# Linear ReLU attention on one Trainium2 core: K's masked copies split in halves, and loads issued seven octets ahead instead of nine

## The chip, the cores and the metric

The kernel runs on one core of one Trainium2 chip. The metric is the device time of one execution in microseconds (us), as the median of several executions.

## The reference

For each of 8 x 12 = 96 heads, with sequence length 512 and head dimension 64, in fp32:

```python
Q_feat = np.maximum(0, Q)
K_feat = np.maximum(0, K)
KV = np.einsum('bhkd,bhkv->bhdv', K_feat, V)
K_sum = np.sum(K_feat, axis=2)
numerator = np.einsum('bhqd,bhdv->bhqv', Q_feat, KV)
denominator = np.einsum('bhqd,bhd->bhq', Q_feat, K_sum)
return numerator / (denominator[:, :, :, None] + 1e-10)
```

## The kernel before

The 96 heads are handled as 12 groups of 8 heads, called octets and numbered 0 to 11. Of each octet, Q, K and V are 1 MB each in HBM (fp32), and so is the output. One transfer moves one of these to or from SBUF, laid out as 128 partitions of 32 rows of 64 numbers. There are thus 36 loads and 12 stores of 1 MB each. The loads of octets 1 to 11, and Q's of octet 0, convert to bf16 on the way; K and V of octet 0 come in fp32 into two buffers that later serve as output buffers.

Two queues issue transfers. GpSimd (POOL) issues nearly all loads, in `load` and `load_q`: K, V, Q of each octet, but K, Q, V for the last one. Its transfers use six semaphores in turn, so each issue waits until the transfer six places earlier has landed. SyncE (SP) issues K and V of octet 0 at the start, and stores. `AHEAD` says how many octets are loaded before the first step; it is also the number of buffers (`NI`) for each of Q, K and V. After that, step i handles the normalisation of octet o = i - 1, then the store of octet o, then the load of octet o + AHEAD + 1 if there is one. `store` (L246) puts the store on POOL's queue, in front of those loads, while there are loads to come; otherwise it goes to SP's queue, and the first of SP's stores waits for K of octet 11 to land. There are seven output buffers (`NOUT`), used in turn, so the normalisation of octet o overwrites the buffer of octet o - 7 and waits for that octet's store to have landed (octets 7 to 11; octets 5 and 6 follow the two buffers that held the fp32 inputs).

Each engine has its own fixed order of instructions, and waits on semaphores that the class `Order` works out from the keys that each operation reads and writes. TensorE (PE) runs a hand-written loop, `products` (L350). In step i, for octet i, with the octet before finished along the way:

1. PE transposes Q of octet i (L360), in two halves; ScalarE (ACT) applies the ReLU to them (L209).
2. PE multiplies K's masked copies with V's (L369), 64 matmuls, the first 32 of which use rows 0 to 15 of the octet's 32 rows (the first half) and the last 32 rows 16 to 31. Each half ends with a signal. ACT copies the product out (L217).
3. PE transposes the previous octet's product back (L378), two halves of 8.
4. PE computes denominators (L354, the form with 16 columns), then the two halves of the numerators (L354, 256 columns). These overwrite the PSUM tiles that step 3 filled, so they wait for VectorE's two normalisations of the previous octet. ACT copies the numerators out (L225; in the last step VectorE takes one half).

VectorE (DVE) in step i, in this order:

- `copy_q(i + 1)` (L206): copies Q of the next octet to the tile that PE transposes; it waits for that Q to land.
- `prep_k(i + 1, 0)` and `prep_k(i + 1, 1)` (L189): ReLU of the next octet's K times a mask, one copy for even and one for odd heads, into the single tile `kf`. Each covers all 32 rows and waits until PE's matmuls of item 2 have read the tile to the end.
- `norm(i - 1, 0)`, `norm(i - 1, 1)` (L239): divides the previous octet's numerators, PSUM to the output buffer.
- three small instructions for the denominators (L230, L234, L237).
- `prep_v` of the next octet (L202), two instructions; ACT does a third (L200).

The key of a K copy stands for a whole copy, which is what makes it wait for both halves of the matmuls:

```python
KF = [[("kf", 0), ("kf", 1), ("vo", 0, j), ("vo", 1, j), "vo1"] for j in range(2)]
```

Of the kernel before, what the change touches and what calls it, by code (L numbers as in the profile page):

```python
# [96 lines left out]
def kernel(  # L97
# [14 lines left out]
    R = S * 4 // P  # L112
# [1 line left out]
    U = RQ // 2  # L114
    NO = NH // 8
    assert NO * 8 == NH and R == 16 and RQ == 32
    AHEAD = 9
    NI = AHEAD
    NOUT = 7
    LANES = 6  # L120
# [16 lines left out]
    mask = sb.tile([P, 2, 2], fp32, name="mask")  # L137
    mask_h = sb.tile([P, 8, 2], fp32, name="mask_h")
    kf = sb.tile([P, RQ, 2, D], bf16, name="kf")
    vo = sb.tile([P, RQ, 2, D4], bf16, name="vo")  # L140
# [22 lines left out]
    def lane(who):  # L163
        turn[who] += 1
        return lanes[who][(turn[who] - 1) % len(lanes[who])]

    do = Order(nc, sems)

    def kv_src(o):
        if o == 0:  # L170
            return (o_sb[0], ("o", 0)), (o_sb[1], ("o", 1))
        return [(x[o % NI].rearrange("p (r d) -> p r d", d=D), (n, o % NI)) for n, x in (("k", k_sb), ("v", v_sb))]
# [6 lines left out]
    def load(o):  # L179
        i = o % NI  # L180
        for n, X, t in (("K", Kr, k_sb), ("V", Vr, v_sb)):
            if n == "V" and o == NO - 1:
                load_q(o)
            do.op("pool", lambda e: e.dma_start(out=t[i], in_=X[o], single_packet=True), writes=[(n.lower(), i)],  # L184
                  dma=lane("pool"))
        if o < NO - 1:
            load_q(o)

    def prep_k(o, s):  # L189
        src, key = kv_src(o)[0]  # L190
        do.op("dve", lambda e: e.tensor_scalar(kf[:, :, s, :], src, scalar1=0.0, scalar2=mask[:, 0, s:s + 1],  # L191
                                               op0=Alu.max, op1=Alu.mult),
              reads=[key, ("mask", 0)], writes=[("kf", s)])

    def prep_v(o, t, halves, who, sem=None):
        src, key = kv_src(o)[1]
        rs = slice(R * halves[0], R * halves[-1] + R)
        to, src, m = vo[:, rs, t, 2:D + 2], src[:, rs], mask[:, 1, t:t + 1]
        if who == "act":
            make = lambda e: e.activation(to, src, Act.Copy, scale=m)  # L200
        else:
            make = lambda e: e.tensor_scalar(to, src, scalar1=m, scalar2=None, op0=Alu.mult)  # L202
        do.op(who, make, reads=[key, ("mask", 1), "vo1"], writes=[("vo", t, j) for j in halves], sem=sem)

    def copy_q(o):
        do.op("dve", lambda e: e.tensor_copy(q2, q_sb[o % NI]), reads=[("q", o % NI)], writes=["q2"], sem="q2")  # L206

    def relu_q(j):
        do.op("act", lambda e: e.activation(qt[:, j * (U // 2):(j + 1) * (U // 2)], ps_qt[j], Act.Relu),  # L209
              reads=[("pq", j)], writes=[("qt", j)])  # L210
# [3 lines left out]
    def evac_kv():  # L214
        for s in range(2):
            for c in range(2):
                do.op("act", lambda e: e.copy(  # L217
                    kvd[64 * c:64 * c + 64, s:8:2, c * D1:c * D1 + D1].rearrange("p (g t) d -> p g t d", t=2),
                    ps_kv[64 * s:64 * s + 64, :, 0:2 * (D + 2)].rearrange(
                        "p g (t d) -> p g t d", t=2)[:, :, :, c:c + D1]),  # L220
                    reads=[("pk", 0), ("pk", 1)], writes=[("kvd", s, c)], sem="ev" if s + c == 2 else None)
# [6 lines left out]
    def denominators():  # L228
        ps = ps_den.rearrange("p (u h c) -> p u (h c)", u=U, h=8)
        do.op("dve", lambda e: e.scalar_tensor_tensor(  # L230
            own.rearrange("p u h c -> p u (h c)"), ps, 1e-10,
            mask_h.rearrange("p h c -> p (h c)").unsqueeze(1).to_broadcast([P, U, 16]), op0=Alu.add, op1=Alu.mult),
            reads=["pd", "mask_h"], writes=["own"])
        do.op("dve", lambda e: e.tensor_reduce(  # L234
            out=den.rearrange("p (u c) -> p u c", c=2), in_=own.rearrange("p u h c -> p u c h"), op=Alu.add,
            axis=mybir.AxisListType.X), reads=["own"], writes=["den"])
        do.op("dve", lambda e: e.reciprocal(rec, den), reads=["den"], writes=["rec"])  # L237

    def norm(o, j):  # L239
        i = (o + 2) % NOUT  # L240
        rs = slice(16 * j, 16 * j + 16)
        do.op("dve", lambda e: e.tensor_tensor(o_sb[i][:, rs], ps_x[j].rearrange("p (r d) -> p r d", d=D),  # L242
                                               rec[:, rs].unsqueeze(2).to_broadcast([P, 16, D]), op=Alu.mult),
              reads=[("x", j), "rec"], writes=[("o", i, j)] if i > 1 else [("o", i, j), ("o", i)], sem=f"n{j}")

    def store(o):  # L246
        i = (o + 2) % NOUT
        to, src = Or[o], o_sb[i].rearrange("p r d -> p (r d)")
        keys = [("o", i, h) for h in range(2)]
        if o + AHEAD + 1 < NO:  # L250
            do.op("pool", lambda e: e.dma_start(out=to, in_=src, single_packet=True), reads=keys, dma=lane("pool"))
        else:
            keys.append(("k", (NO - 1) % NI))
            do.op("sp", lambda e: e.dma_start(out=to, in_=src), reads=keys,
                  dma=lane("sp" if o + NOUT < NO else "last"), kept=o + NOUT >= NO)

    KF = [[("kf", 0), ("kf", 1), ("vo", 0, j), ("vo", 1, j), "vo1"] for j in range(2)]
    PK = [("pk", 0), ("pk", 1)]
    QT = [("qt", 0), ("qt", 1)]
    OT = [("ot", 0), ("ot", 1)]  # L260
# [4 lines left out]
    def body():  # L265
# [12 lines left out]
        for h in range(4):  # L278
            for t in range(2):
                memset("pool", mask[32 * h:32 * h + 32, 1, t:t + 1], 1.0 if h % 2 == t else 0.0,  # L280
                       [("m", h, t), ("mask", 1)])
        for o in range(1, AHEAD + 1):
            load(o)
# [8 lines left out]
    def setup():  # L292
        do.op("dve", lambda e: e.tensor_copy(ident32, ident), reads=["ident"], writes=["ident32"])
        for c in range(2):
            do.op("dve", lambda e: e.tensor_reduce(
                out=mask_h[:, :, c], in_=ident32.rearrange("p (h b) -> p h b", h=8), op=Alu.add,
                axis=mybir.AxisListType.X), reads=["ident32"], writes=[("mh", c), "mask_h"])
        do.op("dve", lambda e: e.tensor_reduce(
            out=mask[:, 0, :], in_=mask_h[:, :, 0].rearrange("p (a s) -> p s a", s=2), op=Alu.add,
            axis=mybir.AxisListType.X), reads=["mask_h"], writes=[("mask", 0)])  # L300
        prep_k(0, 0)
        prep_k(0, 1)
        prep_v(0, 1, (0,), "act", "a0")
        prep_v(0, 0, (0, 1), "dve", "d0")
        prep_v(0, 1, (1,), "dve", "d1")
        do.op("dve", lambda e: e.memset(kvf.bitcast(fp32)[:, 0:4 * D1], 0.0), writes=KVD, sem="n0")
        do.op("dve", lambda e: e.memset(kvf.bitcast(fp32)[:, 4 * D1:], 0.0), writes=KVD, sem="n1")
        copy_q(0)
        for j in range(2):
            nc.scalar.sem_inc(sems[f"t{j}"], 1)  # L310
            do.note("act", "act", (), (), f"t{j}", 1)

    def step(i):
        r = i + 1
        more, last = i + 1 < NO, i == NO

        if not last:
            do.looped([("q2", r)], ["q2", "ident"], [("pq", 0)])
            do.looped([], ["q2", "ident"], [("pq", 1)])
            relu_q(0)  # L320
            relu_q(1)
            do.looped([("a0", r), ("d0", r)], KF[0], PK + ["pd"])
            do.looped([("d1", r)], KF[1], PK + ["pd"])
            evac_kv()
            if more:
                prep_v(i + 1, 1, (0,), "act", "a0")
                copy_q(i + 1)
                prep_k(i + 1, 0)
                prep_k(i + 1, 1)
        if i > 0:  # L330
            o = i - 1
            do.looped([("t0", r), ("t1", r)], [*OT, "ident32"], [("x", 0)])
            do.looped([], [*OT, "ident32"], [("x", 1)])
            for j in range(2):
                norm(o, j)
            store(o)
            if o + AHEAD + 1 < NO:
                load(o + AHEAD + 1)
        if not last:
            do.looped([("ev", r)], [*QT, *KVD], ["pd"])  # L340
            denominators()
            for j in range(2):
                do.looped([(f"n{j}", r)], [*QT, *KVD], [("x", j)])
            copy_ot(0, "act")
            copy_ot(1, "act" if more else "dve")
            if more:
                prep_v(i + 1, 0, (0, 1), "dve", "d0")
                prep_v(i + 1, 1, (1,), "dve", "d1")
# [85 lines left out]
```

## Time and profile before

| | |
|---|---|
| time, median of 3 runs | 125.53 us (125.38 to 125.61) |
| the profiled execution's own time | 125.56 us |
| its span, first to last instruction | 123.7 us |
| mean granted TensorE clock | 0.944 |
| busy, share of span: PE, DVE, ACT, POOL | 69%, 67%, 63%, 22% |
| HBM read, written | 37.75 MB, 12.58 MB: 407 GB/s over the span |
| chain that ended last | DMA 71%, PE 8%, DVE 7%, issue 5%, POOL 4% |

The span is cut in 40 slices of 3.09 us. In the rows of the page each digit is the busy share of one slice in tenths. The row GB/s counts bytes at the SBUF side: a load that turns fp32 into bf16 counts half of what it reads from HBM, so 212 there stands for 424 GB/s read from HBM, while a store counts in full. A row of a group reads: line, engine, operation, tile written and tiles read, shapes, number of instructions, then busy time and mean ns of one, then the engine's idle time in front of them and who ended it.

### The profile page before, as it was taken

Reading aid. Unit: us, or ns where it says so; the run is one execution under the profiler, and the core shown is the slowest. Engines: PE = TensorE matmul, PEld = TensorE weight load, DVE = VectorE, ACT = ScalarE, POOL = GpSimd, SP = SyncE. Lnnn points to the kernel's source line nnn. Section 1 sums busy time; section 2 is a strip of 40 time slices with the busy share of each in tenths; the row PEclk is TensorE's granted clock in tenths of the full one; section 3 lists DMA queues with packets and bytes.
Section 4 is the critical chain, followed back from the end, with each engine's and each line's share of the span. In section 5 each row is a group of like instructions: output and inputs, shape, how many; then the busy total and the mean of one; then the engine's idle time right before and its main releaser. Section 6 shows DMA issues by size and latency. Waiting matters only on the chain.

```text
span 123.7 us, 3402 instructions
## 1 busy us (share of the span) xinstructions
PE 85.0 (69%) x1440; PEld 73.5 (59%) x1440; DVE 82.4 (67%) x127; ACT 78.3 (63%) x108; POOL 27.6 (22%) x55
## 2 busy tenths in 40 slices
PE   0000097697896979969799697996978918983900
PEld 0000096686794867949589485794856916972900
DVE  1261904769789697895987959869688649067330
ACT  0000762998987889878898788987869736652000
POOL 5795311331131213312421142221000000000000
PEclk9999999999999999999999999999999996897555
DMA  3999999999999999999999999999999999999955
GB/s 69 404 315 222 213 215 212 212 212 212 216 215 215 212 212 212 217 215 213 213 215 212 212 212 267 334 215 234 354 217 212 404 424 432 421 421 429 434 238 212
DMA packets 6916, 32.55 MB, mean 263 GB/s; under 512 B 768, under 2 KB 768, under 8 KB 5120
## 3 DMA queue, kind: packets, MB, share of 16 engines
q0 software_dynamic: 5184, 19.93, 75.8%
q1 hardware_dynamic: 1728, 12.58, 24.7%
q14 instruction: 3, 0.02, 0.0%
q8 instruction: 1, 0.02, 0.0%
HBM read 37.75 MB, written 12.58 MB: 407 GB/s over the span
## 4 chain that ended last, share of the span: by engine, by line
DMA 71%; PE 8%; DVE 7%; issue 5%; POOL 4%; POOLq 0%; DVEq 0%; SPq 0%
DMA k_sb<-in_K_dram 54%; DMA q_sb<-in_Q_dram 12%; DMA out_dram<-o_sb 6%; DVE o_sb L242 5%; PE ps_x L378 4%; PE ps_kv L369 2%; POOL vo L263 2%; PE ps_qt L360 1%; DVE ot_sb L225 1%; PE ps_x L354 1%; POOL k_sb L184 1%; POOL mask L263 1%; POOL q_sb L175 1%; POOL v_sb L184 0%; DVE den L234 0%
## 5 line engine op out<-in xcount | busy, mean ns | idle before, releaser
L242 DVE TENSOR_TENSOR o_sb<-ps_x,rec 128x1024 f32<-128x1024 f32 x24 | 28.5, 1217 | 9.2 <-PE ps_x L378 6.6
L225 ACT COPY ot_sb<-ps_x 128x1024 f32<-128x1024 f32 x23 | 23.2, 1013 | 10.7 <-PE ps_x L354 9.8
L369 PE MATMUL ps_kv<-vo,kf 64*128 64x132 bf16 x768 | 26.7, 228 | 0.8 <-DVE vo L202 0.2
L378 PE MATMUL ps_x<-ident,ot_sb 128*128 128x128 f32 x192 | 25.3, 288 | 1.7 <-DVE ot_sb L225 1.7
L369 PEld LDWEIGHTS ps_kv<-vo,kf 64*128 64x128 bf16 x768 | 24.7, 99 | 2.6 <-issue 2.6
L360 PE MATMUL ps_qt<-ident,q 128*128 128x128 bf16 x192 | 14.4, 235 | 16.4 <-DVE q L206 15.4
L209 ACT ACTIVATE qt<-ps_qt 128x1024 bf16<-128x1024 bf16 x24 | 23.4, 1031 | 1.9 <-PE ps_qt L360 1.9
L378 PEld LDWEIGHTS ps_x<-ident,ot_sb 128*128 128x128 f32 x192 | 22.3, 148 | 3.2 <-issue 2.0
L360 PEld LDWEIGHTS ps_qt<-ident,q 128*128 128x128 bf16 x192 | 12.4, 106 | 19.0 <-DVE q L206 15.4
L217 ACT CAST kvd<-ps_kv 64x260 bf16<-64x260 f32 x48 | 17.9, 374 | 8.5 <-PE ps_kv L369 7.6
L354 PE MATMUL ps_x<-qt,kvd 128*128 128x256 bf16 x96 | 14.9, 281 | 12.1 <-DVE o_sb L242 12.0
L191 DVE TENSOR_SCALAR kf<-k_sb,mask 128x2048 bf16<-128x2048 bf16 x22 | 15.6, 750 | 8.5 <-PE ps_kv L369 8.4
L354 PEld LDWEIGHTS ps_x<-qt,kvd 128*128 128x128 bf16 x96 | 7.7, 100 | 16.9 <-DVE o_sb L242 16.3
L206 DVE COPY q<-q_sb 128x2048 bf16<-128x2048 bf16 x12 | 8.2, 686 | 8.6 <-DMA q_sb<-in_Q_dram 8.6
L175 POOL DMA_DIRECT2D q_sb<-in_Q_dram x12 | 9.2, 763 | 19.0 <-DMA q_sb<-in_Q_dram 14.6
L200 ACT ACTIVATE vo<-v_sb,mask 128x1024 bf16<-128x1024 bf16 x11 | 12.7, 1153 | 0.6 <-DMA v_sb<-in_V_dram 0.4
L202 DVE TENSOR_SCALAR vo<-v_sb,mask 128x2048 bf16<-128x2048 bf16 (+1 forms) x22 | 11.6, 568 | 0.0
L184 POOL DMA_DIRECT2D k_sb<-in_K_dram x11 | 7.7, 697 | 16.8 <-DMA k_sb<-in_K_dram 12.9
L184 POOL DMA_DIRECT2D v_sb<-in_V_dram x11 | 6.3, 576 | 16.5 <-DMA v_sb<-in_V_dram 12.7
L200 ACT ACT_TABLE_LOAD x1 | 1.3, 1283 | 12.2 <-DMA o_sb<-in_V_dram 12.2
L354 PE MATMUL ps_kv<-kvd,qt 128*128 128x16 bf16 x192 | 6.9, 179 | 1.7 <-ACT kvd L217 1.7
L354 PEld LDWEIGHTS ps_kv<-kvd,qt 128*128 128x128 bf16 x192 | 6.4, 96 | 2.0 <-ACT kvd L217 1.9
(21 smaller groups left out, 27.6 us busy)
## 6 DMA issues: line engine op xcount, KB each, us to landing
out_dram<-o_sb SPq DMA_DIRECT2D x10, 1024.0 KB, 12.4
q_sb<-in_Q_dram POOLq DMA_DIRECT2D x12, 512.0 KB, 14.5
k_sb<-in_K_dram POOLq DMA_DIRECT2D x11, 512.0 KB, 14.4
v_sb<-in_V_dram POOLq DMA_DIRECT2D x11, 512.0 KB, 14.4
out_dram<-o_sb POOLq DMA_DIRECT2D x2, 1024.0 KB, 14.7
o_sb<-in_K_dram SPq DMA_DIRECT2D x1, 1024.0 KB, 6.2
o_sb<-in_V_dram SPq DMA_DIRECT2D x1, 1024.0 KB, 10.7
```

The source lines that it names most:

```text
L184: do.op("pool", lambda e: e.dma_start(out=t[i], in_=X[o], single_packet=True), writes=[(n.lower(), i)], dma=lane("pool"))
L191: do.op("dve", lambda e: e.tensor_scalar(kf[:, :, s, :], src, scalar1=0.0, scalar2=mask[:, 0, s:s + 1], op0=Alu.max, op1=Alu.mult), reads= ...
L200: make = lambda e: e.activation(to, src, Act.Copy, scale=m)
L202: make = lambda e: e.tensor_scalar(to, src, scalar1=m, scalar2=None, op0=Alu.mult)
L209: do.op("act", lambda e: e.activation(qt[:, j * (U // 2):(j + 1) * (U // 2)], ps_qt[j], Act.Relu), reads=[("pq", j)], writes=[("qt", j)])
L217: do.op("act", lambda e: e.copy(kvd[64 * c:64 * c + 64, s:8:2, c * D1:c * D1 + D1].rearrange("p (g t) d -> p g t d", t=2), ps_kv[64 * s:64 ...
L225: do.op(who, lambda e: e.copy(to, src) if who == "act" else e.tensor_copy(to, src), reads=[("x", j)], writes=[("ot", j)], sem=f"t{j}")
L242: do.op("dve", lambda e: e.tensor_tensor(o_sb[i][:, rs], ps_x[j].rearrange("p (r d) -> p r d", d=D), rec[:, rs].unsqueeze(2).to_broadcast( ...
L354: return pe.matmul(out_, lhsT, rhs, start=True, stop=True, skip_group_check=True)
L360: x = pe.transpose(ps_qt[u // 8][:, u % 8, :], q2[:, u, :], ident)
L369: x = pe.matmul(ps_kv[:, h, 0:2 * (D + 2)].rearrange("p (t d) -> p t d", t=2), kf[ps, R * g + k, :, :].rearrange("p s d -> p (s d)"), vo[p ...
L378: x = pe.transpose(ps_x[u // 8][:, u % 8 * P:u % 8 * P + P], ot[:, u].rearrange("p h c -> p (h c)"), ident32)
```

## The change

The number of octets loaded ahead falls from nine to seven, and with it the number of buffers for Q, K and V. The stores of octets 0 to 3 now go to POOL's queue, each in front of the loads of octets 8 to 11; the stores of octets 4 to 11 go to SP's. Each masked copy of K becomes two instructions of 16 rows. From octet 1 on, the order is: first half for even heads, first half for odd heads, second half for even, second half for odd. The first two wait only for the first half of PE's matmuls of the octet before. For octet 0 the copies stay whole.

```diff
-    AHEAD = 9
+    AHEAD = 7
...
-    def prep_k(o, s):
+    def prep_k(o, s, halves):
         src, key = kv_src(o)[0]
-        do.op("dve", lambda e: e.tensor_scalar(kf[:, :, s, :], src, scalar1=0.0, scalar2=mask[:, 0, s:s + 1],
+        rs = slice(R * halves[0], R * halves[-1] + R)
+        do.op("dve", lambda e: e.tensor_scalar(kf[:, rs, s, :], src[:, rs], scalar1=0.0, scalar2=mask[:, 0, s:s + 1],
                                                op0=Alu.max, op1=Alu.mult),
-              reads=[key, ("mask", 0)], writes=[("kf", s)])
+              reads=[key, ("mask", 0)], writes=[("kf", s, j) for j in halves])
...
-    KF = [[("kf", 0), ("kf", 1), ("vo", 0, j), ("vo", 1, j), "vo1"] for j in range(2)]
+    KF = [[("kf", 0, j), ("kf", 1, j), ("vo", 0, j), ("vo", 1, j), "vo1"] for j in range(2)]
...
-        prep_k(0, 0)
-        prep_k(0, 1)
+        prep_k(0, 0, (0, 1))
+        prep_k(0, 1, (0, 1))
...
-                prep_k(i + 1, 0)
-                prep_k(i + 1, 1)
+                for j in range(2):
+                    for s in range(2):
+                        prep_k(i + 1, s, (j,))
```

The order of transfers on the two queues, where a number is an octet, L its three loads and S its store:

| | POOL | SP, after K of octet 11 has landed |
|---|---|---|
| before | Q of 0, L1 to L9, S0, L10, S1, L11 | S2 to S11 |
| after | Q of 0, L1 to L7, S0, L8, S1, L9, S2, L10, S3, L11 | S4 to S11 |

## The prediction

> **What bounds the kernel now.** The first thing to read is the slices of the page. DMA is at 9 from the second slice to the 38th.
>
> ```profile
> DMA  3999999999999999999999999999999999999955
> GB/s 69 404 315 222 213 215 212 212 212 212 216 215 215 212 212 212 217 215 213 213 215 212 212 212 267 334 215 234 354 217 212 404 424 432 421 421 429 434 238 212
> out_dram<-o_sb SPq DMA_DIRECT2D x10, 1024.0 KB, 12.4
> ```
>
> Loads run at 212, which is 424 GB/s out of HBM; the stores at the end run at 421 to 434. So one transfer of 1 MB costs the same, whichever it is, and the kernel is 48 of them behind one another. The second view is POOL's timeline, where an issue tells the landing of the transfer six places earlier:
>
> ```profile
> 73.52 0.92 POOL L175 DMA_DIRECT2D q_sb<-in_Q_dram  x1 [1.70 <-DMA k_sb<-in_K_dram]
> 75.95 0.54 POOL L251 DMA_DIRECT2D out_dram<-o_sb  x1 [1.51 <-DMA v_sb<-in_V_dram]
> 78.40 0.83 POOL L184 DMA_DIRECT2D k_sb<-in_K_dram  x1 [1.92 <-DMA q_sb<-in_Q_dram]
> 80.90 0.53 POOL L175 DMA_DIRECT2D q_sb<-in_Q_dram  x1 [1.67 <-DMA out_dram<-o_sb]
> ```
>
> The distance is 2.43 to 2.50, also across a store; I take 2.46. The third view is the chain that ended last, at the place where loads give way to stores:
>
> ```profile
> 78.40 14.85 DMA k_sb<-in_K_dram
> 93.25 0.02 issue
> 93.27 7.43 DMA out_dram<-o_sb
> 100.70 0.02 issue
> 100.72 2.37 DVE o_sb L242 x2
> ```
>
> K of octet 11 lands at 93.25. Behind it stand Q and V of octet 11 and ten stores, 12 x 2.46 = 29.5, so the transfers cannot end before 122.8. The last store is issued at 118.9 (the trace gives its landing as 3.8 later), so it lands at 122.7: the transfers are a floor on which the kernel already lies. The compute reaches the same point with next to nothing to spare. Octet 11's last normalisation ends at N = 117.68 + 1.23 = 118.91 (VectorE's timeline), and the time is 125.56, so time = N + 6.65 once the compute is what is late. The profiled execution's 125.56 is 0.03 above the median, so sums on its trace stand for the median.
>
> What happens before N is read from VectorE's timeline:
>
> ```profile
> 82.70 2.35 DVE L242 TENSOR_TENSOR o_sb<-ps_x,rec 128x1024 f32<-128x1024 f32 x2
> 88.42 0.69 DVE L206 COPY q<-q_sb 128x2048 bf16<-128x2048 bf16 x1 [1.23 <-DMA q_sb<-in_Q_dram]
> 95.78 0.69 DVE L206 COPY q<-q_sb 128x2048 bf16<-128x2048 bf16 x1 [0.44 <-DMA q_sb<-in_Q_dram]
> 97.19 1.42 DVE L191 TENSOR_SCALAR kf<-k_sb,mask 128x2048 bf16<-128x2048 bf16 x2 [0.72 <-PE ps_kv L369]
> 100.72 2.35 DVE L242 TENSOR_TENSOR o_sb<-ps_x,rec 128x1024 f32<-128x1024 f32 x2 [2.11 <-DMA out_dram<-o_sb]
> ```
>
> Octet 9's normalisation waits 2.11 us for a buffer, until octet 2's store lands at 100.70. The change takes away this wait, since that store moves among the loads. What is late next is the question.
>
> **Loads, part one of the change.** Octet 8's loads get one store more in front of them, those of octets 9, 10 and 11 two more (before: none, one, two in front of 9, 10, 11; after: two, three, four). So Q of octet 10 lands 2 x 2.46 = 4.92 later and its copy starts at 88.42 + 4.92 = 93.34; Q of octet 11 is copied at 95.78 + 4.92 = 100.70. The moved stores themselves cost nothing: their data is ready long before (octet 3's normalisation runs at 51.7, its store would be issued near 81), and none is late for its buffer. The floor does not move: K of octet 11 at 98.17, then ten transfers, 122.8 again. So the removed wait buys nothing on the side of the transfers; if this cover were gone, it would have been worth the 2.11.
>
> **Copies of K, part two.** Four instructions of 1024 elements take the place of two of 2048. The two now hold VectorE for 1.33 (81.37 to the next start at 82.70). No row has the half. From below, half the work at half the time leaves 1.33 for the four; from above, each half costs a whole, 2.68. The nearest rows are V's copies:
>
> ```profile
> L191 DVE TENSOR_SCALAR kf<-k_sb,mask 128x2048 bf16<-128x2048 bf16 x22 | 15.6, 750 | 8.5 <-PE ps_kv L369 8.4
> L202 DVE TENSOR_SCALAR vo<-v_sb,mask 128x2048 bf16<-128x2048 bf16 x11 | 7.2, 657 | 0.0
> L202 DVE TENSOR_SCALAR vo<-v_sb,mask 128x1024 bf16<-128x1024 bf16 x11 | 5.3, 478 | 0.0
> ```
>
> There a half saves 0.18, which would make 0.67 - 0.18 = 0.49; the fp32 forms of the same line (1287 and 746) save 42%, which makes 0.39. I take 0.45, four for 1.80, 0.47 more than now. [...]
>
> In return the first two halves start when PE has done half of its matmuls, 1 us earlier. In steps 1 to 6 this makes the compute a little faster (now 7.68 an octet, 75.0 to 82.70), but Q lands every 7.4 us, and from octet 8 on at 73.3, 83.2, 93.3 and 100.7. Nothing gained before lasts past those landings; I cost this at nothing.
>
> **The sum.** Step 9 now starts with Q of octet 10: copy at 93.34, K's halves from 93.97 (0.63 as at 88.42 to 89.05; PE's matmuls are done by then) to 95.77, normalisation of octet 8 at 95.77. From an unhindered normalisation to the end of the next K and V matmuls it is 6.24 (82.70 to 88.94): 102.01. PE then needs 0.98 for half its transposes and 0.1 to signal: 103.1. On VectorE, Q of octet 11 is copied at 100.70, K's first halves run 101.33 to 102.23, its second halves, free from 102.1, to 103.13. By both ways octet 9's normalisation starts at 103.1 instead of 100.72: it no longer waits for a store, it stands behind the copies of a Q that lands 4.9 later.
>
> From there to N it is 118.91 - 100.72 = 18.19 now. Two stretches at half clock are in it:
>
> ```profile
> 99.53:102.94 3.41, 0.61 (x4) 0.31 (x4) 2.22 (x2) 1.06 (x2) 0.00 (x0) 1.00 1.01 428
> 102.94:106.35 3.41, 3.21 (x32) 2.72 (x34) 2.21 (x6) 2.87 (x4) 0.00 (x0) 0.50 1.00 423
> 109.77:113.18 3.41, 1.88 (x27) 1.17 (x24) 3.34 (x6) 1.01 (x1) 0.00 (x0) 1.00 1.00 423
> 113.18:116.60 3.42, 2.60 (x13) 2.63 (x14) 1.22 (x2) 0.00 (x0) 0.00 (x0) 0.50 1.01 424
> ```
>
> The columns are the stretch, its length, busy PE, PEld, DVE, ACT and POOL, then the granted clock. A stretch of 3.41 in which PE is busy for 0.61, or for 1.88, is followed by one at 0.50. The first costs 7.32 (100.72 to 108.04) against 6.24, so 1.08; the second makes the last transposes 3.65 long instead of 1.97, so 1.68. At full clock the way to N is 15.43.
>
> After the change the first gap is gone from this place, as PE has Q-bound work right up to 103; the second stays, since it is PE's wait for denominators and copies in the last step. N = 103.13 + 15.43 + 1.68 = 120.24; time 126.89, say **126.9 us**, 1.3 more than now.
>
> **The rivals.** *Both gaps cost.* In step 9 PE waits for octet 8's normalisation, from about 94.5 (octet 7's starts at 83.2 + 0.63 + 1.80 = 85.6; 6.24 for octet 9's matmuls, 1.97 for the transposes, 0.6 for the denominators) to 97.0 (95.77 + 1.27, as 82.70 to 83.97), as long as the 2.54 before 102.00, and half clock after that can hit octet 10's matmuls, which lie on the path, for up to 1.08: 128.0. For it: the same gap did this above. Against: the stretch may fall on work that Q's landing covers.
>
> *No gap costs, the floor holds.* Then N = 118.56, time 125.2, under the floor, so 125.56, no change. This needs the last transposes to fall outside a half-clock stretch, which depends on where the 3.41 us stretches begin. [...]
>
> *Faster.* The one way is through the floor: stores among loads must be cheaper than stores alone, and the compute not late. If each of the two moved stores took 2.2 instead of 2.46, all would end 0.5 earlier, 125.05; it decides from 0.13 for each on. Against: the issue rows above show 2.45 and 2.50 around a store.
>
> **How the numbers follow.** Chances: one gap costs (126.4 to 127.4) 0.50; both (127.4 to 128.8) 0.29; floor 0.17; faster 0.04. The half copies' bounds move octet 9's normalisation by -0.46 (0.335 each) to +0.87 (0.67 each). The range runs from just under the floor, 125.4, to both gaps with somewhat dearer halves, 128.3. A measurement tells about 0.2% from no change, 0.25 us: faster 0.04, same 0.17, slower 0.79.
>
> **What would show it.** Right: waits of the Q copies on DMA near 73, 83, 93 and 100.7; no wait of a normalisation on a store; octet 9's normalisation near 103; a half K copy near 0.5; DMA below 9 in the slices before the last store. Wrong: octet 9's normalisation before 102 (the step from Q's landing fails), a distance under 2.4 between issues around stores (the floor fails), full clock in the last transposes (the floor rival), or V of octet 11 landing after about 105, which would put ACT on the path.

## The result, and the profile after

The changed kernel takes 127.21 us (median of six executions, 126.06 to 128.79), the kernel before 125.57 beside it (125.35 to 125.92). The ratio is 1.012, with a 95% interval of 1.0096 to 1.0143: the change made the kernel slower by 1.2%. A ratio leaves out executions over 1.5% above a kernel's fastest (one here, four of twelve for seven octets ahead alone), while the medians in this document are over all.

The profiled execution is the fastest of the six: 126.06, with a span of 124.2. It shows the smallest loss, not the median's. First the slices of the page, as shown for the kernel before:

```profile
DMA  2999999999999999999999999999999999999945
GB/s 58 400 317 230 214 214 211 212 214 214 214 212 216 214 214 211 211 216 215 233 360 211 214 375 218 211 365 233 214 331 264 211 301 417 425 427 425 427 203 211
out_dram<-o_sb SPq DMA_DIRECT2D x8, 1024.0 KB, 10.5
```

The four stores on POOL's queue are now the four peaks among the loads (360, 375, 365, 331); the stretch of pure stores at the end is shorter. The DMA engines are as busy as before. POOL's timeline has the same distances, also around a store:

```profile
78.60 0.53 POOL L175 DMA_DIRECT2D q_sb<-in_Q_dram  x1 [1.88 <-DMA k_sb<-in_K_dram]
81.11 0.54 POOL L252 DMA_DIRECT2D out_dram<-o_sb  x1 [1.98 <-DMA v_sb<-in_V_dram]
83.55 0.62 POOL L184 DMA_DIRECT2D k_sb<-in_K_dram  x1 [1.90 <-DMA q_sb<-in_Q_dram]
86.02 0.53 POOL L175 DMA_DIRECT2D q_sb<-in_Q_dram  x1 [1.85 <-DMA out_dram<-o_sb]
```

They are 2.44 to 2.51. VectorE's timeline shows what octet 9's normalisation now stands behind:

```profile
83.35 0.69 DVE L207 COPY q<-q_sb 128x2048 bf16<-128x2048 bf16 x1 [3.01 <-DMA q_sb<-in_Q_dram]
...
93.19 0.69 DVE L207 COPY q<-q_sb 128x2048 bf16<-128x2048 bf16 x1 [3.15 <-DMA q_sb<-in_Q_dram]
...
101.00 0.69 DVE L207 COPY q<-q_sb 128x2048 bf16<-128x2048 bf16 x1 [1.14 <-DMA q_sb<-in_Q_dram]
101.61 1.67 DVE L192 TENSOR_SCALAR kf<-k_sb,mask 128x1024 bf16<-128x1024 bf16 x4
103.20 2.35 DVE L243 TENSOR_TENSOR o_sb<-ps_x,rec 128x1024 f32<-128x1024 f32 x2
```

There is no wait on a store any more. In its place the engine waits for Q of octets 9, 10 and 11, and the normalisation at 103.20 follows the copies without idle time. The chain that ended last says the same (a piece of the chain begins where its releaser ends, so its times differ a little from the timeline's):

```profile
86.02 14.89 DMA q_sb<-in_Q_dram
100.91 0.03 issue
...
101.61 1.67 DVE kf L192 x4
103.28 2.27 DVE o_sb L243 x2
...
115.39 2.78 PE ps_x L380 x16
118.16 0.02 issue
118.19 1.23 DVE o_sb L243
```

Before, a landing store stood at that place in the chain, at 100.70; now it is Q of octet 11 at 100.91. N, the end of the last normalisation, is 118.19 + 1.23 = 119.42 against 118.91.

### The profile page after: what moved, and what is told of

Read it like the earlier page. It is cut to its first block, busy times and chain, and to the rows that moved or that the text cites. A ratio compares the mean times of both kernels' runs of the same rounds, so it can differ in the third digit from the quotient of the medians.

```text
span 124.2 us, 3423 instructions
## 1 busy us (share of the span) xinstructions
PE 87.1 (70%) x1440; PEld 75.6 (61%) x1440; DVE 85.9 (69%) x149; ACT 78.4 (63%) x108; POOL 26.8 (22%) x57
## 4 chain that ended last, share of the span: by engine, by line
DMA 79%; DVE 8%; PE 6%; issue 3%; DVEq 0%; POOLq 0%; SPq 0%
DMA q_sb<-in_Q_dram 55%; DMA v_sb<-in_V_dram 12%; DMA out_dram<-o_sb 12%; DVE o_sb L243 5%; PE ps_x L380 3%; PE ps_kv L371 2%; DVE kf L192 1%; DVE ot_sb L226 1%; PE ps_qt L362 1%; PE ps_x L356 0%; DVE den L235 0%; DVE rec L238 0%; DVE own L231 0%; DVE q L207 0%; DVEq L73 0%
## 5 line engine op out<-in xcount | busy, mean ns | idle before, releaser
L371 PE MATMUL ps_kv<-vo,kf 64*128 64x132 bf16 x768 | 28.7, 238 | 0.5
L371 PEld LDWEIGHTS ps_kv<-vo,kf 64*128 64x128 bf16 x768 | 26.8, 104 | 2.4 <-issue 2.4
L362 PE MATMUL ps_qt<-ident,q 128*128 128x128 bf16 x192 | 15.6, 247 | 16.8 <-DVE q L207 15.7
L380 PE MATMUL ps_x<-ident,ot_sb 128*128 128x128 f32 x192 | 24.4, 282 | 1.7 <-DVE ot_sb L226 1.7
L362 PEld LDWEIGHTS ps_qt<-ident,q 128*128 128x128 bf16 x192 | 13.4, 112 | 19.5 <-DVE q L207 15.7
L380 PEld LDWEIGHTS ps_x<-ident,ot_sb 128*128 128x128 f32 x192 | 21.4, 143 | 3.2 <-issue 2.0
L192 DVE TENSOR_SCALAR kf<-k_sb,mask 128x1024 bf16<-128x1024 bf16 x44 | 19.0, 482 | 2.8 <-PE ps_kv L371 2.4
L175 POOL DMA_DIRECT2D q_sb<-in_Q_dram x12 | 7.2, 603 | 18.8 <-DMA q_sb<-in_Q_dram 10.5
L184 POOL DMA_DIRECT2D v_sb<-in_V_dram x11 | 7.2, 651 | 17.1 <-DMA v_sb<-in_V_dram 9.6
L184 POOL DMA_DIRECT2D k_sb<-in_K_dram x11 | 7.0, 633 | 17.6 <-DMA k_sb<-in_K_dram 9.8
```

The source lines that it names most:

```text
L192: do.op("dve", lambda e: e.tensor_scalar(kf[:, rs, s, :], src[:, rs], scalar1=0.0, scalar2=mask[:, 0, s:s + 1], op0=Alu.max, op1=Alu.mult) ...
L362: x = pe.transpose(ps_qt[u // 8][:, u % 8, :], q2[:, u, :], ident)
L371: x = pe.matmul(ps_kv[:, h, 0:2 * (D + 2)].rearrange("p (t d) -> p t d", t=2), kf[ps, R * g + k, :, :].rearrange("p s d -> p (s d)"), vo[p ...
L380: x = pe.transpose(ps_x[u // 8][:, u % 8 * P:u % 8 * P + P], ot[:, u].rearrange("p h c -> p (h c)"), ident32)
```

## The experiments

The theory: two more stores in front of the loads of octets 9 to 11 make Q land 4.9 later; its copies stand in front of the previous normalisation in VectorE's queue, so the compute ends after the transfers; gaps of TensorE that come with it halve its clock (0.50 granted instead of 1.00) and add to that. The rivals: the half copies cost; the fewer buffers cost; the transfers alone decide.

**Halves alone** (nine octets ahead, K's copies in halves).

```diff
-    AHEAD = 7
+    AHEAD = 9
```

> The changed kernel with nine octets loaded ahead, as before: only K's copies are in halves. Theory (the late landing of Q of octets 10 and 11, behind two more stores, is what costs): Q lands as before the change, octet 9's normalisation waits for octet 2's store at 100.7 again, and the end lies on the transfers' floor: 125.5 (125.3 to 125.9), no change from before. Rival (the halves cost: 22 more VectorE instructions, 3.4 us more busy time in all): at least 0.25 per octet over the last steps, 126.0 to 127.2.

Measured: 125.73 (125.58 to 126.46, 12 executions), ratio to the kernel before 1.0016, interval 0.9996 to 1.0037. The normalisation waits for the store again (it starts at 100.82), and N is 115.04 + 2.35 = 117.39:

```profile
100.82 2.35 DVE L243 TENSOR_TENSOR o_sb<-ps_x,rec 128x1024 f32<-128x1024 f32 x2 [1.92 <-DMA out_dram<-o_sb]
115.04 2.35 DVE L243 TENSOR_TENSOR o_sb<-ps_x,rec 128x1024 f32<-128x1024 f32 x2 [1.32 <-PE ps_x L380]
```

The halves alone neither cost nor gain anything that can be told. N fell by 1.5, most of it because the last transposes ended earlier: VectorE waits 1.32 for them here, and its last two normalisations run in one piece; in the kernel before it waits 2.20 and then another 0.41, and the transposes take 3.65. That the time did not fall with it shows the floor. The last store of this profile is a second sign:

```profile
DMA to landing us min/median/max: 5.5/5.5/5.5
```

In the profile of before it takes 3.8 from its issue to its landing. Here it had to wait for the stores in front.

**Seven octets ahead alone** (K's copies whole).

```diff
-    AHEAD = 9
+    AHEAD = 7
```

> The kernel before with seven octets loaded ahead: K's copies stay whole. Theory: Q of octet 11 is copied near 101.0, K's whole copies follow once PE has ended octet 10's matmuls near 101.7, and octet 9's normalisation starts near 103.1, as in the changed kernel (103.2): 127.0 (126.0 to 127.7). Rival (the halves cost): 125.5.

Measured: 126.96 (125.66 to 128.31, 12 executions). The loss is there without the halves. The ratio is 1.006 (1.0019 to 1.010); the medians give 126.96 / 125.58 = 1.011. The profile (126.62) has Q of octet 11 copied at 100.79, as expected, and the normalisation later than expected:

```profile
98.46 1.88 PE L360 MATMUL ps_qt<-ident,q 128*128 128x128 bf16 x16
100.27 2.61 PE L369 MATMUL ps_kv<-vo,kf 64*128 64x132 bf16 x64
```

```profile
102.93 1.42 DVE L191 TENSOR_SCALAR kf<-k_sb,mask 128x2048 bf16<-128x2048 bf16 x2 [1.45 <-PE ps_kv L369]
104.26 2.35 DVE L242 TENSOR_TENSOR o_sb<-ps_x,rec 128x1024 f32<-128x1024 f32 x2
...
117.63 2.35 DVE L242 TENSOR_TENSOR o_sb<-ps_x,rec 128x1024 f32<-128x1024 f32 x2 [1.32 <-PE ps_x L378]
```

TensorE's transposes take 1.88 instead of 1.06 and its matmuls 2.61 instead of 2.07: a half-clock stretch lies on octet 10's work, and K's copies wait 1.45 for that, not for Q. It is the first gap of the prediction's rival "both gaps cost". From octet 9's normalisation on this execution shows no such delay: the last normalisations start 13.37 later, against 13.36 in the changed kernel's profile (103.20 to 116.56), where the clock is 1.00 up to 116.3, and they run in one piece. I take it for full clock. That way takes 117.63 + 2.35 - 104.26 = 15.72.

**Seven buffers, but two stores among the loads.** Octets 2's and 3's stores are recorded behind octet 11's loads, on SP's queue.

```diff
-        if o + AHEAD + 1 < NO:
+        if o < 2:
             do.op("pool", lambda e: e.dma_start(out=to, in_=src, single_packet=True), reads=keys, dma=lane("pool"))
...
-            store(o)
+            if o not in (2, 3):
+                store(o)
             if o + AHEAD + 1 < NO:
                 load(o + AHEAD + 1)
+            if o == 3:
+                store(2)
+                store(3)
```

> The changed kernel (seven octets ahead, seven buffers, halves), but octets 2's and 3's stores go to SyncE's queue behind the loads, so that two stores stand among the loads, as before the change. Theory: Q of octet 11 lands near 95.7, octet 9's normalisation waits for octet 2's store near 100.7, the end is on the floor: 125.5 (125.3 to 125.9). Rival (fewer buffers or another place of them is what costs): 126.5 to 127.5, as the changed kernel.

Measured: 126.02 (125.72 to 126.78), ratio 1.0046 (1.0023 to 1.0069). Most of the loss is gone with the same number of buffers, so they are not what costs most of it. One thing was not foreseen: the two stores stand in front of octets 8 and 9 here, so Q of octet 9 is copied at 83.69 instead of 79.42, and octet 9's normalisation starts at 102.16, held up by the compute since then, with octet 9's transposes at 1.88 instead of 1.06 and its matmuls at 2.78 instead of 2.07 (from 89.05 on), as at half clock, and not by Q of octet 11. This does not explain the 0.4 that are left: in the same profile (126.03) N is 115.53 + 2.36 = 117.89, 1.0 under that of the kernel before, and the last store lands near 123.2, 5.3 after that (an estimate: the span ends at 124.2, and where the last landing is shown, it lies 0.9 to 1.0 ahead of that end), so there the transfers decide. Why they end later than before (118.9 + 3.8 = 122.7) stays open.

**Eight octets ahead**, three stores among the loads.

```diff
-    AHEAD = 7
+    AHEAD = 8
```

> The changed kernel with eight octets ahead: three stores among the loads, nine behind. Theory: Q of octet 11 lands near 98.3, octet 2's store is landed in time, octet 9's normalisation starts near 100.6, so N lies between 116.0 (full clock) and 118.8 and the floor decides: 125.4 (125.2 to 126.0). Rival (each store moved costs the same, half of the change's 1.6): 126.3. Rival (stores among loads are cheaper): under 125.2.

Measured: 126.03 (125.57 to 127.14), ratio 1.0034 (1.0007 to 1.0061): between the floor and half of the loss. In the profile (125.94) Q of octet 11 is copied at 98.51 and N is 117.68, under that of the kernel before, while the last store needs 5.3 to land: the floor decides that execution. The longer ones, up to 127.14, have no profile.

**Six octets ahead**, five stores among the loads (with the end's waits restricted to the semaphores in use).

```diff
-    AHEAD = 7
+    AHEAD = 6
```

> The changed kernel with six octets ahead: five stores among the loads, seven behind. Theory (once Q of octet 11 lands too late, every further store in front of it costs its whole 2.46): Q of octet 11 is copied near 103.5, K's four halves take 1.6, octet 9's normalisation starts near 105.7, N is 121.1 at full clock and up to 2.8 more: about 129.6, 2.4 above the changed kernel's median of 127.2. Rival (the loss comes from where the stores are, not from Q's landing): near 127.2.

Measured: 129.54 (128.76 to 131.53), 2.3 above the changed kernel's 127.21. In the profile:

```profile
103.44 0.69 DVE L207 COPY q<-q_sb 128x2048 bf16<-128x2048 bf16 x1 [0.71 <-DMA q_sb<-in_Q_dram]
104.10 1.83 DVE L192 TENSOR_SCALAR kf<-k_sb,mask 128x1024 bf16<-128x1024 bf16 x4
106.06 2.36 DVE L243 TENSOR_TENSOR o_sb<-ps_x,rec 128x1024 f32<-128x1024 f32 x2
```

One store more in front is 2.44 more for Q of octet 11. With two, three, four and five stores among the loads, halves in all, the medians run 125.73, 126.03, 127.21 and 129.54: nearly flat at the floor, then 1.2 for the fourth store and 2.3, nearly a whole transfer, for the fifth.

**The last gap filled.** In the last step TensorE transposes the identity 24 times in front of the last transposes.

```diff
                     if h % 4 == 3:
                         x.then_inc(sems["pe"], 1)
+                with pe.If(r > NO - 1):
+                    for k in range(24):
+                        pe.transpose(ps_qt[k // 8 % 2][:, k % 8, :], ident, ident)
```

> The changed kernel, and in the last step TensorE does 24 idle transposes of the identity, which nobody reads, in the gap in front of the last transposes. Theory (the gap puts the clock at half for the last transposes, up to 1.68): the last transposes take 1.97 and N is near 118.7, so most runs lie between the floor and 0.6 above it: median 126.1 against 127.2. Rival (half clock plays no part): 127.2.

Measured: 127.37 (126.06 to 128.81). The last transposes ran at 1.94 in the profile, as expected, and the median did not fall: this expectation failed. In the profile (126.06, the fastest of the six) octet 10's transposes took 1.54 from 98.93, instead of 1.06, as with half clock on a part of them, and octet 9's normalisation started at 103.53. The idle work is not free either: from there to N it is 117.05 + 2.36 - 103.53 = 15.88, against 15.72 without it.

**All gaps from step 7 on filled**, with 14 more behind the denominators.

```diff
+                with pe.If(r > 7):
+                    for k in range(14):
+                        pe.transpose(ps_qt[k // 8][:, k % 8, :], ident, ident)
                 q = qt.rearrange("p u (h c) -> p u h c", h=8)
```

> As the run before, and from step 7 on 14 more idle transposes in each step, behind the denominators, where TensorE waits for VectorE's normalisation. Theory (half clock after those gaps makes octet 10's matmuls late in some runs): no half clock from 75 on, octet 9's normalisation at 103.2 and N near 118.7 in every run: 125.8 (125.4 to 126.2), with a smaller spread than the run before. Rival (Q's landing alone is late, no half clock before the last step): the same as the run before.

Measured: 126.31 (125.97 to 128.17), 0.9 under the changed kernel and 1.1 under the run before, but half a microsecond over what was expected; the spread is 2.2 against 2.75, and the executions of the two runs overlap. In the profile (125.97) the granted clock is 1.00 from 92.0 to 106.4 and from 113.0 to beyond N = 119.02, and octet 11's matmuls in between take 2.07. So filling these gaps takes away about half of the loss at the median, with an uncertain size. Two more executions of this kernel, on another chip, have a profile each.

> The changed kernel with idle transposes in the gaps from step 7 on, once more, for a look at what still spreads its times (125.97 to 128.17). Theory (half clock): if this run is over 126.8, a half-clock stretch after 90 lies on octet 10's or 11's matmuls or on the last transposes; if it is under 126.4, none does. Rival (the landings spread): over 126.8 with full clock after 90, and Q of octet 10 or 11 copied over 0.5 later than 93.4 and 100.6.

> The same kernel as in the run before, for a second look: over 126.8 with a half-clock stretch on the path after 90 (theory), or over 126.8 at full clock with later landings of Q (rival).

Measured: 126.30 and 126.41, in both octet 10's and 11's matmuls at 2.07 and the last transposes at 1.94, as at full clock. Q of octet 11 is copied at 101.48 and 101.46 instead of 100.56, and N is 119.58 and 119.77 instead of 119.02. These two thus differ from the first by Q's landing, 0.9 later, which makes N 0.56 and 0.75 later. The two agree with each other within 0.02 in the landing, and ran on another chip than the first, so the record cannot tell the chip from the execution. Neither was over 126.8, so what makes the executions up to 128.17 long stays open: they had no profile.

**The floor lowered.** Eight octets ahead, halves, the last gap filled, one store less.

```diff
-            store(o)
+            if o != 5:
+                store(o)
```

> Eight octets ahead, halves, the idle transposes in the last step, and octet 5's store left out, so that there is one transfer less in the queue; the compute is unchanged. Theory (with eight octets ahead the transfers are the floor, 2.46 each): 2.0 to 2.5 less than the 126.0 with eight octets ahead, 123.5 to 124.0. Rival (the compute is what ends late, the transfers follow it): 125.3 or more.

Measured: 124.25 (123.34 to 125.35), 1.8 under eight octets ahead with all stores. Two things differ from that run, the store and the idle transposes, and N tells them apart: between the two profiles N fell by 0.55 (117.68 to 117.13) and the time by 2.13 (125.94 to 123.81). With three stores among the loads the transfers were the bound, and one transfer less takes most of a transfer's 2.46 away. In the profile (123.81) the last store lands 3.8 after its issue and N + 6.65 = 117.13 + 6.65 = 123.78: the compute has become the bound again.

**The changed kernel again.**

> The changed kernel once more, beside the next run. Theory: 127.2 at the median (126.0 to 128.0 with the place of the half-clock stretches), the profile again with Q of octet 11 copied near 101 and octet 9's normalisation at 103.2 or later. Rival (its 127.2 belonged to the chip it ran on): 125.8 or less.

Measured: 127.72 (126.65 to 128.50). The loss is there again. This profile took 127.91, and shows what the first one lacks. Q of octet 11 lands as before, yet the normalisation starts at 104.47:

```profile
100.79 0.69 DVE L207 COPY q<-q_sb 128x2048 bf16<-128x2048 bf16 x1 [0.61 <-DMA q_sb<-in_Q_dram]
102.41 0.88 DVE L192 TENSOR_SCALAR kf<-k_sb,mask 128x1024 bf16<-128x1024 bf16 x2 [0.93 <-PE ps_kv L371]
103.46 0.88 DVE L192 TENSOR_SCALAR kf<-k_sb,mask 128x1024 bf16<-128x1024 bf16 x2 [0.17 <-PE ps_kv L371]
104.47 2.36 DVE L243 TENSOR_TENSOR o_sb<-ps_x,rec 128x1024 f32<-128x1024 f32 x2
```

The busy times in stretches cut along the clock's steps (columns: stretch, length, busy PE, PEld, DVE, ACT, POOL, granted clock, DMA, GB/s), this profile first:

```profile
95.60:99.00 3.40, 1.59 (x19) 0.90 (x16) 3.33 (x6) 1.92 (x3) 0.00 (x0) 1.00 1.06 210
99.00:102.50 3.50, 3.50 (x56) 3.30 (x55) 1.96 (x5) 2.61 (x3) 0.00 (x0) 0.51 1.06 280
112.70:116.10 3.40, 1.63 (x24) 0.92 (x20) 3.33 (x6) 1.01 (x1) 0.00 (x0) 1.00 1.00 422
116.10:119.50 3.40, 2.83 (x14) 2.86 (x15) 1.20 (x2) 0.00 (x0) 0.00 (x0) 0.50 0.78 330
```

and the profile of 126.06:

```profile
95.90:99.30 3.40, 2.03 (x23) 1.44 (x24) 3.33 (x6) 2.04 (x3) 0.00 (x0) 1.00 1.05 208
99.30:102.70 3.40, 3.34 (x79) 3.08 (x77) 2.26 (x6) 2.92 (x6) 0.00 (x0) 1.00 1.05 301
112.90:116.30 3.40, 1.52 (x13) 1.26 (x14) 2.27 (x5) 0.68 (x1) 0.00 (x0) 1.00 1.02 429
116.30:119.70 3.40, 1.85 (x10) 1.45 (x8) 2.45 (x2) 0.00 (x0) 0.00 (x0) 0.50 0.66 280
```

The same program, the same gaps. With 1.59 of TensorE's work in the stretch from 95.6, the next one runs at half clock and octet 10's matmuls take 2.99 instead of 2.07; with 2.03 in it, they run at full clock. At the end the last transposes take 3.32 in the one and 2.76 in the other, against 1.94 at full clock. That is 104.47 - 103.20 = 1.27 at the first place and 3.32 - 2.76 = 0.56 at the second, together 1.83 of the 1.85 between the two executions.

**Q first.** Of octets 8 to 11, Q is loaded in front of K and V.

```diff
         for n, X, t in (("K", Kr, k_sb), ("V", Vr, v_sb)):
-            if n == "V" and o == NO - 1:
+            if n == "K" and o > AHEAD:
                 load_q(o)
...
-        if o < NO - 1:
+        if o <= AHEAD:
             load_q(o)
```

> The changed kernel with one thing moved: of octets 8 to 11 Q is loaded in front of K and V (it was behind them for 8 to 10 and between them for 11); four stores stay among the loads. Theory (the late landings of Q hold up VectorE's queue): Q of octet 10 lands near 88.3 and K near 90.8, octet 8's normalisation starts near 92.5 instead of 95.4; K of octet 11 lands near 101.0 and octet 9's normalisation starts at 102.7, now with 3 of slack for octet 10's matmuls, so that a half-clock stretch there costs nothing: 126.3, 0.9 less than the changed kernel beside it. Rival (the order of the three does not matter, the store's place does): the same as the changed kernel, within 0.3.

Measured: 127.00 (125.73 to 128.87, 12 executions), 0.7 under the changed kernel beside it, which ranges from 126.65 to 128.50; with these spreads it is not settled whether the order gains anything. The 126.3 that was expected did not come. The starts came as expected, octet 8's normalisation at 92.78 and octet 9's at 102.75. But its profile, of one of the longer executions (127.86), has octet 11's matmuls at 2.98 instead of 2.07 (from 107.50) and the last transposes at 3.59 instead of 1.94, as at half clock, N = 121.21: the gaps moved with the work.

No version that stores all twelve octets beat the kernel before: those with the earliest N (117.39 to 117.89) lie on the floor.

## Why the prediction was right, and where it was not

The number was 126.9, the range 125.4 to 128.3, the sign slower; measured 127.21. Step by step:

- *Loads.* Copies of Q were put at 73.3, 83.2, 93.3 and 100.7; they start at 73.54, 83.35, 93.19 and 101.00. Transfers of 2.46, stores among them, held. (The prediction's 7.68 an octet is the distance from 44.05 to 51.73 in VectorE's rows; from 74.89 to 82.70 it is 7.81. Nothing rests on it.)
- *The removed wait buys nothing.* The wait on octet 2's store is gone, and Q of octet 11 with the copies behind it is what is late next. Octet 9's normalisation was put at 103.13 and starts at 103.20.
- *Half copies.* Four were put at 1.80 and take 1.59 (101.61 to 103.20), 0.40 each, by the row of the fp32 forms rather than the middle that I took; the row reads 482 ns. The 0.2 too much cancelled against Q's landing 0.3 later: that the start of the normalisation came out within 0.1 is in part luck. That the halves by themselves cost nothing is shown by the halves alone; whether they cost some tenths together with seven octets ahead (126.96 without, 127.21 and 127.72 with) is not settled.
- *The floor.* Shown by the halves alone (N down by 1.5, the time not), and by the store left out. The relation time = N + 6.65 holds: 126.06 - 119.42 = 6.64. With six octets ahead it is more, 128.76 - 121.72 = 7.04, and with all gaps filled, 125.97 - 119.02 = 6.95, which nothing here explains.
- *The term that was mis-sized: half clock.* The sum had 15.43 for the way from octet 9's normalisation to N at full clock, 1.68 for half clock at the last transposes, and none before them. At full clock the way takes 15.72 with seven octets ahead alone and 15.73 with eight (101.95 to 117.68). VectorE's last two normalisations take their 2.35 one behind the other there, so transposes that end earlier do not move the second one up by as much. Half clock there had thus cost 18.19 - 1.08 - 15.72 = 1.39 before the change; the two errors of 0.29 cancel in the sum.
- *What it measured after the change.* In the profile of 126.06 half clock costs 119.42 - 103.20 - 15.72 = 0.50, all at the last transposes. In that of 127.91 it costs 1.27 at octet 10, and N = 118.72 + 2.53 = 121.25, so 121.25 - 104.47 - 15.72 = 1.06 at the last transposes. The second is the rival "both gaps cost", put at 128.0 with a chance of 0.29; no profile shows the one full gap that the 126.9 was made of. The median lies between the two, and that 126.9 came so close to it is luck.
- *What half clock is to the loss.* At full clock the changed kernel would take 103.20 + 15.72 + 6.65 = 125.57, an estimate from these profiles, which is the time of the kernel before. Octet 9's normalisation starts 2.48 later than before. Without half clock the compute of before would have ended 1.08 + 1.39 = 2.47 earlier, so that much of it could hide in front of the floor. The later start has used this up, and now time at half clock, and a later landing in some executions, shows in the time in full.
- *The reason given for the gaps.* The prediction judged the gaps by their length, about 2.5 as before the change, although its own rows show that a stretch with 1.88 of work was enough for half clock. In step 9 the gap was put at 2.5, from 94.5 to 97.0; it is only 1.07 in the one profile and 1.19 in the other, since half clock in the step before had made octet 9's matmuls late (3.09 and 2.73 instead of 2.07), and 1.19 was enough.

## What to carry to other kernels

A store moved from behind the loads to among them took nothing from the transfers here (the issues stood 2.44 to 2.51 apart, also around a store); it delayed the loads behind it by one transfer (Q of octet 11 by 2.44 for the fifth store), so move only as many as the compute at the end has slack for. When a wait is removed, look at what stands in front of the waiting instruction in its engine's queue: here the next octet's Q, landing about 5 later, replaced a wait of 2.1. And when a kernel becomes bound by arrivals, the gaps they leave on TensorE can cost a second time: 1.27 at octet 10 in one execution here, nothing there in another.

## What was not expected of the hardware

In the profiles of the kernel before and of the changed kernel (126.06), half clock goes with how long TensorE was busy in the stretch of 3.41 ahead of it, and not with the length of a gap. They were cut along the steps of the granted clock, from 35 us to the end of the work. The full-clock stretches followed by one at 0.50 had 0.61 and 1.88 busy before the change (from 99.53 and 109.77) and 1.12, 1.79 and 1.55 after it (from 75.37, 85.61 and 112.91). The other full-clock stretches, each followed by one at 1.00, had 2.31 or more before and 1.99 or more after (the rows shown above are cut at rounded times and have 2.03 and 1.52 for 1.99 and 1.55). The second profile of the changed kernel has 1.59 and 1.63, both followed by 0.50. No sharp limit is shown: ahead of those 35 us, a stretch with 1.81 (the kernel before, from 21.02) was followed by full clock.

Behind the same gap of 1.73 the last transposes took 3.65 in the kernel before, 2.76 and 3.32 in the changed kernel, and 1.94 with six octets ahead. A gap of 1.19 was enough for half clock where the stretch held only 1.59 of work (the changed kernel again), and one of 2.02 passed (the last of the filled kernel's profiles, up to 97.65; the transposes behind it take 1.06 and the matmuls 2.07). Where the stretches begin against the work differs from execution to execution: octet 8's normalisation starts 0.47 ahead of the stretch from 95.85 in the first profile of the changed kernel (95.38), and 0.1 behind the start of the stretch from 95.6 in the second (95.69). Between these two executions half clock made 1.83 of 1.85; how much of the changed kernel's whole range, 126.1 to 128.8, it makes is not shown.
